# A hybrid decoder block on one core: attention's beginning in a written order, running sums as rows of the logits' product, and three smaller moves

## The chip, the cores and the metric

The kernel runs on one core of a Trainium2 chip. A core has a matrix engine (TensorE, PE in the profile, with its weight loads shown apart as PEld), a vector engine (DVE), an activation engine (ACT), a general engine (POOL), a queue engine that issues transfers (SP), and 16 DMA engines. Engines run their instructions in order and wait for each other by semaphores. The metric is the device time of one execution in microseconds; lower is better.

## The reference

One layer of a decoder block on 1024 tokens of width 1024, in float32. Cut to what matters here:

```python
def forgetting_attention(q, k, v, log_f):
    c = jnp.cumsum(log_f, axis=1)                       # running sum per head
    ...
    logits = jnp.einsum('bqhd,bkhd->bhqk', qi, k) * scale
    logits = logits + ci[..., None] - c_k
    logits = jnp.where(causal, logits, -jnp.inf)
    p = jax.nn.softmax(logits, axis=-1)
    return jnp.einsum('bhqk,bkhd->bqhd', p, v)

def chunked_spatial_gating(u, vg, v_gain, w_s, b_s):
    vg = rmsnorm(vg, v_gain.reshape(G, Dg))
    w = w_s * jnp.tril(jnp.ones((CHUNK, CHUNK)))
    mixed = jnp.einsum('gij,bnjgd->bnigd', w, vc) + b_s.T[None, None, :, :, None]
    return u * mixed

xn = rmsnorm(h, norm_mix_g);  proj = xn @ w_in          # q, k, v, u, gate, forget logits
att = forgetting_attention(q, k, v, log_sigmoid(forget + b_forget))
sg = chunked_spatial_gating(gelu(u), gelu(gate), ...)
h = h + concat([att, sg]) @ w_out
h = h + conv_ffn(rmsnorm(h), w_up, conv_w, conv_b, w_down)   # 1024 -> 2*2816 -> 1024
return rmsnorm(h, norm_final_g)
```

There are 8 attention heads of 64 and 8 gating groups of 64.

## The kernel before

**Numbers in two halves.** A float32 value is split into a rounded high part and the rest (`split_w`: ACT casts the high part, DVE or POOL subtracts). A product is then three products: high by high, high by low, low by high. Large products (512 columns a matmul) are in addition computed by Strassen-Winograd steps on halves (the names A11, S1 to S4, T1 to T4 and so on).

**Stages.** Gate and value projections come first, then queries and keys of head pairs (`qk_step`, four steps), the rest of the values (`tmul` and `tprod` into four accumulator banks `S`, lines 729 to 732), the spatial gate (`spatial`, line 679, called at 733), attention, the output product (`wmm`, line 1019), the up projection with convolution, the down projection, and the last norm (`finish`, line 1426).

**Order.** Python emits instructions in program order and a scheduler gives each engine its queue; it may let a ready instruction pass an earlier one that is not. Three devices restrict it. `Line` wraps ACT and DVE: while `on` is true every call is ordered behind the one before on that engine. `seq` chains TensorE's instructions in attention. `after` orders one instruction behind another.

**Spatial gate.** Eight groups, three matmuls each into one bank (lines 690 to 692); DVE adds the bias and multiplies by `u`, two instructions a group, one for each half of the tokens (sixteen of 128x256). `turn_sg(hf)` (line 699) then transposes a half of the result on TensorE into four banks (line 705), ACT casts the high part (707), DVE subtracts the low part (708). Those are the `G` tiles that the output product of the gate reads.

**Attention.** For head h and query tile j (128 queries against (j+1)x128 keys), `logits(h, j)` (line 776):
- POOL's `affine_select` (786) copies the running sums of the last 512 keys with the causal mask into the place of the result; for the other keys the sums are read from `cks`, a copy of the head's row on all 128 partitions.
- For each 512 keys two matmuls into one bank (793, 794): rows (q high, q low) by (k high, k low), and the same rows by (k low, k high). There are four such banks (tag "s").
- DVE adds the sums to the bank and takes the running minimum, one instruction for each 512 keys (796; the kernel keeps the logits negated, so the minimum is the softmax's maximum).
- ACT takes the exponential with the row sum (799).

`turn_p` transposes two key tiles of the result into a bank (812), ACT casts (813), DVE subtracts (814). `values` multiplies them with V (831) and adds the two halves (839, 840). `row_tail(h)` takes the reciprocal of the row sums on DVE (738), transposes it (739), copies it (740) and sends it through memory to be spread. `pair_half` multiplies a pair of heads with it on POOL (752 to 754) and splits the result for the output product.

A head is five steps of two transposed groups. In step s of head h the values of head h and the logits of head h+1 are computed (`NEXT`), and the transposes of the next step are emitted ahead. `FILLS` names the steps after which one **filler** is emitted: a token tile of the gate's part of the output product (`sg_out`, 12 matmuls, lines 873 to 875, sixteen in all), with its own load, addition (876) and store. Fillers use the four "b" banks, which the transposes and values use too. `head_loads(h)` issues a head's transfers two heads ahead; the output weights of attention are loaded and split on POOL by `wo_load` (898, 899) in head 7's program place, ordered behind selects and loads of head 6.

**Last norm.** `finish(tt, done)`: ACT takes the root of the mean square, DVE the reciprocal (1432), ACT scales one half of the row (1434), DVE the other half with the gain (1435), SP stores the tile (1437). It runs for tiles 4 to 7 after the last product.

Of the kernel before, what the change touches and what calls it, by code (L numbers as in the profile page):

```python
# [14 lines left out]
P = 128  # L15
# [5 lines left out]
FILLS = {(-1, j): 1 for j in (5, 3, 0)} | {(h, s): 1 for h in range(5) for s in ((0, 2, 4), (1, 3))[h % 2]}  # L21
# [44 lines left out]
def block_kernel(ctx: ExitStack, tc: tile.TileContext, xT, xtok, wuv, wv, wqk, wf, cpk, bfv,  # L66
# [76 lines left out]
    ncd = drm.tile([8, 1024], F32, name="ncd")  # L143
# [108 lines left out]
    def tmul(banks, w, n, k, first, apart=False):  # L252

        ops = [(m, c) for m in range(4) for c in range(3)]
        for m, c in sorted(ops, key=lambda o: (o[1] > 0, o)) if apart else ops:
            ms = slice(m * P, (m + 1) * P)
            xi, wi = ((0, 0), (0, 1), (1, 0))[c]
            pe.matmul(banks[m], xs(n, xi, k)[:, ms], w[:, wi, :], start=(first and k == 0 and c == 0),
                      stop=(k == 3 and c == 2), skip_group_check=True)
# [196 lines left out]
    def forget():  # L456
# [4 lines left out]
        bfb, z, e, rows = c[:, 136:144], c[:, 144:208], c[:, 208:272], c[0:64, 272:400]  # L461
        tri, ones, lh, ll = r[:, 0:P], r[:, P:2 * P], r[:, 256:320], r[:, 320:384]
# [7 lines left out]
        act.copy(ones, one128)  # L470
        dve.scalar_tensor_tensor(out=tri, in0=maskb, scalar=0.0, in1=ident, op0=ALU.is_gt, op1=ALU.add)
# [18 lines left out]
    def forget_sums(c, r, zr):  # L490
        sel, bfb, z, e, rows = c[0:64, 128:136], c[:, 136:144], c[:, 144:208], c[:, 208:272], c[0:64, 272:400]
# [25 lines left out]
        def turn():  # L517
            pe.transpose(ps[0:64, 192:320], z, ident)
            act.activation(rows, ps[0:64, 192:320], AF.Copy, scale=-1.0)
            sp.dma_start(out=ncd.rearrange("h (t p) -> (h t) p", p=P), in_=rows)  # L520
# [47 lines left out]
    def qk_step(i, qa, nxt):  # L568
# [22 lines left out]
        if i < 2:  # L591
            gate_part(0, 2 * i)
# [16 lines left out]
        emit(tq, qd, i, -0.125, (hi,))  # L609
        return qa  # L610
# [68 lines left out]
    def spatial():  # L679
# [5 lines left out]
        ws = [sb("wy", [P, 8, P], F32R) for _ in range(2)]  # L685
        split_w(wr, ws)
        for g in range(8):
# [5 lines left out]
            for hf in range(2):  # L693
                u3 = ut[hf][:, :, g * 64:(g + 1) * 64]
                dve.scalar_tensor_tensor(out=u3, in0=ps[:, hf * 256:(hf + 1) * 256].rearrange("p (t d) -> p t d", d=64),
                                         scalar=bs[:, g:g + 1], in1=u3, op0=ALU.add, op1=ALU.mult)

    def turn_sg(hf):

        for c in range(4):  # L700
            if hf == 0:
                sgT[c] = sb("G", [P, 2, 1024], F32R)
            ps = bank()
            for t in range(4):
                seq(pe.transpose(ps[:, t * P:(t + 1) * P], ut[hf][:, t, c * P:(c + 1) * P], ident))
            o = slice(hf * 512, hf * 512 + 512)
            act.copy(sgT[c][:, 0, o], ps)
            dve.tensor_tensor(out=sgT[c][:, 1, o], in0=ps, in1=f32(sgT[c][:, 0, o]), op=ALU.subtract)

    S = [sbank() for _ in range(4)]  # L710
    for k in range(4):
        tmul(S, w0[k], "T3", k, True)
        pool.tensor_tensor(out=wvr[k][:, 1, :], in0=wvr[k][:, 0, :], in1=wvr[k][:, 1, :], op=ALU.add)
    tprod(S, lambda k: wvr[k][:, 1, :], "B22", False)
    spatial()
    for m in range(4):
        evac_v(4 + m, S[m])

    act.activation(pad[:, 0:1], eps, AF.Exp)
    act.last = dve.last = None  # L720
# [7 lines left out]
    loads = [None] * 8  # L728
    exs = []
    rows = [None] * 8  # L730
    sels = [[] for _ in range(8)]

    def row_tail(h):
# [3 lines left out]
        rt = sb("t01", [8, P])  # L737
        dve.reciprocal(rs, rs)
# [6 lines left out]
    def pair_half(p, o):  # L745
# [4 lines left out]
        if p < 3:  # L750
            s = sels[2 * p + 3][o.start // 512 * 3:]
# [761 lines left out]
```

## Time and profile before

| what | value |
|---|---|
| time, median of 3 runs (range) | 1075.26 us (1074.52 to 1075.49) |
| the profiled execution's own time | 1075.26 us |
| its span, first to last instruction | 1073.5 us |
| granted TensorE clock, mean | 0.998 |
| ACT, POOL busy share | 53%, 23% |
| DMA moved | 160.80 MB, mean 150 GB/s |

A row of the timeline has the start, the length, the engine, the line, the operation, output from input with shapes, and in brackets the engine's idle time before it with what released it. Consecutive equal instructions are merged (x12). A row of the stretches has the length and then the busy time of PE, PEld, DVE, ACT and POOL (number of instructions), the granted clock, the DMA share and GB/s. Matmul ends are modelled, so a row can overlap its successor; the distance from start to start is the rate.

### The profile page before, as it was taken

The page shows a single profiled execution, that of the slowest core. Times are in us where ns is not written, and L with a number is a line of the kernel's source. Part 1 is how long each engine was busy: PE and PEld are TensorE (multiplying, and loading weights), DVE is VectorE, ACT ScalarE, POOL GpSimd, SP SyncE. Part 2 cuts the span into 40 slices and gives each one's busy share as a digit, 9 for nine tenths or more (in the row PEclk, how much of TensorE's full clock was granted, in tenths as well). Part 3 has the DMA queues.
Part 4 walks back from the last instruction along what each step waited for, and adds up shares of the span by engine and source line. Part 5 has one row for each costly group of instructions (what it writes and reads, how often), then busy time and mean ns, then how long its engine had stood idle before and what let it go on. Part 6 is the DMA issues. An engine that isn't in the chain of part 4 may idle for free.

```text
span 1073.5 us, 14486 instructions
## 1 busy us (share of the span) xinstructions
PE 1055.4 (98%) x5013; PEld 875.3 (82%) x5013; DVE 897.1 (84%) x1367; ACT 570.7 (53%) x985; POOL 245.6 (23%) x219
## 2 busy tenths in 40 slices
PE   9999999999999899999999999999999999999997
PEld 7888788778888788878888888888888888888886
DVE  5986798787877869999899988989988776898774
ACT  6666644466666755764444444444344444454653
POOL 0002134131316630054333333333322000000000
PEclk9999999999999999999999999999999999999999
DMA  9243267956547425132245413222331899433442
GB/s 339 96 137 100 69 159 213 266 189 204 179 167 235 130 89 197 68 117 91 101 135 170 164 69 128 99 99 98 107 118 48 289 323 323 123 94 97 143 123 96
DMA packets 66297, 160.80 MB, mean 150 GB/s; under 512 B 7976, under 2 KB 8240, under 8 KB 66224
## 3 DMA queue, kind: packets, MB, share of 16 engines
q1 hardware_dynamic: 65792, 159.32, 45.6%
q8 instruction: 39, 0.64, 0.2%
q10 hardware_dynamic: 432, 0.57, 0.1%
q14 instruction: 34, 0.28, 0.1%
HBM read 117.06 MB, written 42.80 MB: 149 GB/s over the span
## 4 chain that ended last, share of the span: by engine, by line
PE 74%; DVE 3%; DMA 2%; issue 1%; ACT 1%; POOL 0%; POOLq 0%; DVEq 0%; ACTq 0%; SPq 0%
PE k L1366 20%; PE qa L1114 11%; PE qc L1114 11%; PE qd L1114 11%; PE qb L1114 5%; PE pb L831 3%; PE pb L812 2%; PE pf L873 1%; PE ps L793 1%; PE pf L875 1%; PE ps L794 1%; PE pf L874 1%; PE pb L1023 1%; PE pb L1025 1%; PE pb L1024 1%
## 5 line engine op out<-in xcount | busy, mean ns | idle before, releaser
L1366 PE MATMUL k<-whb,wha 128*128 128x512 f32 x924 | 209.7, 389 | 0.0
L1366 PEld LDWEIGHTS k<-whb,wha 128*128 128x128 f32 x924 | 173.3, 188 | 36.2 <-DVE wha L160 0.2
L1114 PE MATMUL qc<-xT,whb 128*128 128x512 f32 x540 | 129.8, 389 | 0.0
L1114 PE MATMUL qa<-xB,wha 128*128 128x512 f32 x528 | 127.3, 390 | 0.0
L1114 PEld LDWEIGHTS qc<-xT,whb 128*128 128x128 f32 x540 | 101.3, 188 | 21.2 <-ACT whb L154 0.2
L1114 PEld LDWEIGHTS qa<-xB,wha 128*128 128x128 f32 x528 | 98.8, 188 | 20.8 <-DVE wha L160 0.4
L154 ACT CAST wha<-sg 128x512 fp32r<-128x512 f32 x77 | 47.8, 622 | 96.9 <-PE k L1366 86.4
L154 ACT CAST whb<-sg 128x512 fp32r<-128x512 f32 x82 | 50.6, 618 | 86.0 <-PE qc L1114 69.0
L160 DVE TENSOR_TENSOR wha<-sg,wha 128x512 fp32r<-128x512 f32 x77 | 52.8, 688 | 40.4 <-ACT wha L154 40.3
L1114 PE MATMUL qd<-xB,whb 128*128 128x512 f32 x264 | 63.9, 389 | 0.5 <-DVE h L1233 0.5
L1114 PE MATMUL qd<-xT,whb 128*128 128x512 f32 x264 | 63.6, 389 | 0.0
L1001 POOL TENSOR_TENSOR sg<-raw 128x512 f32<-128x512 f32 x20 | 31.2, 1562 | 136.5 <-DVE whb L160 75.7
L160 DVE TENSOR_TENSOR whb<-sg,whb 128x512 fp32r<-128x512 f32 x82 | 58.3, 711 | 4.4 <-ACT whb L154 4.3
L1114 PE MATMUL qb<-xT,whb 128*128 128x512 f32 x252 | 60.9, 389 | 0.0
L814 DVE TENSOR_TENSOR pt<-pb,pt 128x512 fp32r<-128x512 f32 (+1 forms) x80 | 49.9, 634 | 11.4 <-ACT pt L813 10.9
L1114 PEld LDWEIGHTS qd<-xB,whb 128*128 128x128 f32 x264 | 49.5, 188 | 11.2 <-issue 0.9
L1114 PEld LDWEIGHTS qd<-xT,whb 128*128 128x128 f32 x264 | 49.5, 188 | 10.3
L1114 PEld LDWEIGHTS qb<-xT,whb 128*128 128x128 f32 x252 | 47.3, 188 | 9.8
L813 ACT CAST pt<-pb 128x512 fp32r<-128x512 f32 (+1 forms) x80 | 42.4, 539 | 20.7 <-PE pb L812 13.5
L831 PE MATMUL pb<-pt,V 128*128 128x256 f32 x320 | 51.5, 285 | 0.9 <-DVE pt L814 0.8
L1004 POOL TENSOR_TENSOR sg<-sg,raw 128x512 f32<-128x512 f32 x20 | 33.4, 1670 | 64.3 <-DVE whb L160 64.3
L831 PEld LDWEIGHTS pb<-pt,V 128*128 128x128 f32 x320 | 44.1, 189 | 3.3 <-PE pb L812 1.1
(401 smaller groups left out, 2298.8 us busy)
## 6 DMA issues: line engine op xcount, KB each, us to landing
raw<-wup SPq DMA_DIRECT2D x44, 512.0 KB, 3.7
sg<-hx SPq DMA_DIRECT2D x77, 256.0 KB, 2.7
hx<-hs SPq DMA_DIRECT2D x44, 256.0 KB, 3.6
hx<-ca SPq DMA_DIRECT2D x35, 256.0 KB, 2.3
xT<-wdn SPq DMA_DIRECT2D x28, 256.0 KB, 4.0
raw<-wqk SPq DMA_DIRECT2D x8, 512.0 KB, 4.7
qd<-G SPq DMA_DIRECT2D x16, 256.0 KB, 3.2
kd<-G SPq DMA_DIRECT2D x16, 256.0 KB, 3.8
```

The lines of the kernel that those rows point to most:

```text
L154: act.copy(h, src)
L160: return eng.tensor_tensor(out=l, in0=src, in1=f32(h), op=ALU.subtract)
L793: seq(pe.matmul(ps[:, 0:e - c], A[:, qs], B[:, c:e], start=True, stop=False))
L794: seq(pe.matmul(ps[:, 0:e - c], A[:, qs], B2[:, c:e], start=False, stop=True))
L812: seq(pe.transpose(ptr[:, c:c + P], tj[jj][:, k * P:(k + 1) * P], ident))
L813: act.copy(pt[:, 0, 0:w], ptr[:, 0:w])
L814: dve.tensor_tensor(out=pt[:, 1, 0:w], in0=ptr[:, 0:w], in1=f32(pt[:, 0, 0:w]), op=ALU.subtract)
L831: seq(pe.matmul(po[0][:, oo:oo + n], lhs, pt[:, s, o:o + n], start=(k == 0 and s == 0), stop=(s == 1 and half)))
L1001: pool.tensor_tensor(out=s[0], in0=a21, in1=a22, op=ALU.add)
L1004: pool.tensor_tensor(out=s[3], in0=s[1], in1=a12, op=ALU.add)
L1114: pe.matmul(ps, w[:, wi, ks], xb[:, xi, k, :], start=(first and n == 0), stop=(n == 11), skip_group_check=True)
L1366: pe.matmul(banks[bk + m], xh[:, xi, ms], wh[:, wi, :], start=(first and p_ == 0 and n == 0), stop=(p_ == NP - 1 and n == 2), skip_group_c ...
```

## The change

**Values' bank order.** The first eight blocks of the values' product no longer go bank by bank for each k: banks 0 to 2 take k = 0 and 1 first, then bank 3.

**Gate's norm.** `gate_part(0, 2)` (a square on ACT, a reduction and two 1024-wide products on DVE) moves from the middle of `qk_step(1)` to its end.

**Running sums as rows.** The negated sums are stored as high and low rows, and a row pair of ones beside them. A logit's two matmuls become (q high, q low) by (k high, k high), and (q high, 1, 1) by (k low, sums high, sums low), 66 rows deep. The product of the low parts of q and k is left out. `cks`, its broadcast load and POOL's selects go. A constant mask (bfloat16: zeros, and at its end the triangle of large numbers) is added instead. The bank pool is laid out anew for attention: four "b" banks and two places "L" of two banks each; a tile's logits, whatever their width, take one place, and one DVE instruction reads them.

**The beginning.** Loads of head 0 are issued ahead of the values' last product. From `spatial` to the first logits the order of ACT and DVE is written out. The V parts are taken from the banks ahead of the gate; DVE multiplies the first half of the tokens, ACT adds the bias to the second half and POOL multiplies it; the splits of the filler's weights stand between the groups, on ACT and POOL.

**Heads.** Fillers stand after steps 0, 2, 4 of head 0 and 1, 4 of heads 1 to 5. The reciprocal of `row_tail` is taken ahead of the second minimum of the next head, its transposes after the step's first values. POOL's work on pairs and output weights is ordered behind no select any more. After attention the bank pool is laid out a third time, and the first products of the output go half by half.

**Last root.** For tile 6, `finish` scales its half on POOL instead of ACT.

```diff
-FILLS = {(-1, j): 1 for j in (5, 3, 0)} | {(h, s): 1 for h in range(5) for s in ((0, 2, 4), (1, 3))[h % 2]}
+FILLS = {(-1, j): 1 for j in (5, 3, 0)} | {(h, s): 1 for h in range(6) for s in ((0, 2, 4) if h == 0 else (1, 4))}
...
+        sp.dma_start(out=oned.rearrange("s (t p) -> (s t) p", p=P), in_=f32(ones[0:16, :]))
...
+            rh, rl = r[0:64, 0:P], r[0:64, P:2 * P]
+            act.activation(rh, ps[0:64, 192:320], AF.Copy, scale=-1.0)
+            dve.scalar_tensor_tensor(out=rl, in0=ps[0:64, 192:320], scalar=-1.0, in1=f32(rh),
+                                     op0=ALU.mult, op1=ALU.subtract)
+            for s, t in enumerate((rh, rl)):
+                sp.dma_start(out=ncd[s].rearrange("h (t p) -> (h t) p", p=P), in_=f32(t))
...
-        if i < 2:
-            gate_part(0, 2 * i)
+        if i == 0:
+            gate_part(0, 0)
...
+        if i == 1:
+            gate_part(0, 2)
...
+        act.on = dve.on = True
         split_w(wr, ws)
+        act.activation(pad[:, 0:1], eps, AF.Exp)
+        for m in range(4):
+            evac_v(4 + m, S[m])
+        tmp = [sb("pt", [P, 4, 256]) for _ in range(2)]
         for g in range(8):
...
+            dve.scalar_tensor_tensor(out=u[0], in0=v3(ps[:, 0:256]), scalar=bs[:, g:g + 1], in1=u[0],
+                                     op0=ALU.add, op1=ALU.mult)
+            t = tmp[g // 4][:, g % 4, :]
+            act.activation(t, ps[:, 256:512], AF.Identity, bias=bs[:, g:g + 1])
+            pool.tensor_tensor(out=u[1], in0=v3(t), in1=u[1], op=ALU.mult)
+            if g in parts:
+                parts[g]()
...
+    for k, ms_ in ((0, range(3)), (1, range(3)), (0, (3,)), (1, (3,)), (2, range(4)), (3, range(4))):
+        tmul(S, w0[k], "T3", k, True, ms_=ms_)
...
+        sp.dma_start(out=f32(ab[:, 0, :]), in_=qd[h].rearrange("s d t -> (s d) t"))
+        for s in range(2):
+            sp.dma_start(out=f32(ab[s * 64:s * 64 + 64, 1, :]), in_=kd[h, 0])
+        sp.dma_start(out=f32(a2s[0:64, hh, :]), in_=qd[h, 0])
+        if h < 2:
+            sp.dma_start(out=f32(a2s[64:66, hh, :]), in_=oned)
+        sp.dma_start(out=f32(b2s[64:66, hh, :]), in_=ncd[:, h, :])
+        loads[h] = sp.dma_start(out=f32(b2s[0:64, hh, :]), in_=kd[h, 1])
...
+    head_loads(0)
     tprod(S, lambda k: wvr[k][:, 1, :], "B22", False)
...
+    spatial({3: early_split, 5: early_split})
...
+    psa.release()
+    psa = tc.alloc_tile_pool(name="psb", bufs=4, space=bass.MemoryType.PSUM, reuse_waits="tile")
+    def place():
+        return psa.tile([P, 1024], F32, tag="L", bufs=2, name=nm("pl"))
...
+            seq(pe.matmul(ps[:, c:e], A[:, qs], B[:, c:e], start=True, stop=False))
+            seq(pe.matmul(ps[:, c:e], A2[:, qs], B2[:, c:e], start=False, stop=True))
...
+        m = dve.tensor_tensor_reduce(out=places[h, i][jj], in0=ps[:, 0:n], in1=msk[:, 1024 - n:1024], scale=1.0,
+                                     scalar=lim[:, 0:1], op0=ALU.add, op1=ALU.min, accum_out=mn)
+        if h and j == 6:
+            after(tc, m, recips[h - 1])
...
-    turn_sg(0)
-    for j in range(7, -1, -1):
+    for c in range(4):
+        ps = turn_sg(0, c)
+        sg_hi(0, c, ps)
+        sg_lo(0, c, ps)
+        if c % 2:
+            early_split()
+    for j in (7, 6):
+        logits_mm(0, j, firsts[j])
+    pts = [turn_sg(1, c) for c in range(4)]
+    for c in range(4):
+        sg_hi(1, c, pts[c])
+    m7 = logits_min(0, 7, firsts[7])
+    sg_lo(1, 0, pts[0])
+    sg_lo(1, 1, pts[1])
+    m6 = logits_min(0, 6, firsts[6])
+    sg_lo(1, 2, pts[2])
+    logits_exp(0, 7, m7)
+    logits_exp(0, 6, m6)
+    logits(0, 5)
+    sg_lo(1, 3, pts[3])
+    act.on = dve.on = False
...
+            if s == 1 and c == (h == 7):
+                row_tail(h)
...
+    psa.release()
+    psa = tc.alloc_tile_pool(name="psc", bufs=4, space=bass.MemoryType.PSUM, reuse_waits="tile")
...
-    for tt in first:
-        for hf in range(2):
+    for hf in range(2):
+        for tt in first:
             wmm(tt, hf, banks8[tt, hf], (0, 1, 2))
...
+        if tt == 6:
+            pool.tensor_tensor(out=y[tt][:, done], in0=y[tt][:, done], in1=r.to_broadcast((P, 512)), op=ALU.mult)
+        else:
+            act.activation(y[tt][:, done], y[tt][:, done], AF.Copy, scale=r)
```

180 lines of the change are left out of this document (82 added, 98 removed).

## The prediction

> **What bounds the kernel now.** I read the page's first block, the busy time by stretch, then the timelines of each engine around the stretches where TensorE is not full.
>
> ```profile
> span 1073.5 us, 14486 instructions
> PE 1055.4 (98%) x5013; PEld 875.3 (82%) x5013; DVE 897.1 (84%) x1367; ACT 570.7 (53%) x985; POOL 245.6 (23%) x219
> ...
> 500.00:520.00 20.00, 20.00 (x90) 16.42 (x89) 16.41 (x18) 9.11 (x14) 6.79 (x5) 1.00 0.23 79
> ```
>
> TensorE sets the end: 18.1 us of idle in the whole span. In a full stretch 90 matmuls of 512 columns take 20 us, 0.222 us each, so one filler (12 of them) is worth 2.67 us. From about 400 us to the last matmul PE is full, so what is won before 400 us moves the end by as much. Almost all idle lies in two places, the beginning of attention and the heads. The beginning on PE, and what ACT, DVE and POOL do beside it (start, us, engine, line, idle before):
>
> ```profile
> 194.07 3.69 PE L258 MATMUL ps<-wy,x 128*128 128x512 f32 x15 [0.83 <-DVE G L44]
> ...
> 203.04 5.63 PE L258 MATMUL ps<-wy,t 128*128 128x512 f32 x24
> ...
> 219.39 1.81 PE L705 MATMUL pb<-ident,A 128*128 128x128 f32 x12
> 221.36 0.63 PE L705 MATMUL pb<-ident,A 128*128 128x128 f32 x4 [0.15 <-DVE A L44]
> ...
> 223.56 1.91 PE L705 MATMUL pb<-ident,A 128*128 128x128 f32 x16
> 225.25 0.50 PE L793 MATMUL ps<-x 128*128 128x512 f32 x1
> ...
> 227.74 0.50 PE L873 MATMUL pf<-whl,G 128*128 128x512 f32 x1 [1.31 <-DVE G L708]
> ...
> 238.01 1.80 PE L812 MATMUL pb<-ident,t 128*128 128x128 f32 x15
> ```
> ```profile
> 212.11 2.73 ACT L44 ACTIVATE V<-ps,rstd 128x512 fp32r<-128x512 f32 x4 [4.45 <-PE ps L258]
> 220.03 0.59 ACT L707 CAST G<-pb 128x512 fp32r<-128x512 f32 x1 [5.19 <-PE pb L705]
> ...
> 236.52 0.49 ACT L799 ACTIVATE gg<-gg,mn 128x256 f32<-128x256 f32 x1
> ```
> ```profile
> 202.34 1.28 DVE L44 TENSOR_TENSOR wy<-raw,wy 128x512 fp32r<-128x512 f32 x2
> ...
> 214.86 6.35 DVE L44 SCALAR_TENSOR_TENSOR A<-pb,cp,A 128x256 f32<-128x256 f32 x16
> ...
> 225.79 0.74 DVE L796 CUSTOM_DVE_ANT_0 t<-ps,t,mn 128x512 f32<-128x512 f32 x1
> ...
> 226.46 0.61 DVE L796 CUSTOM_DVE_ANT_0 t<-ps,t,mn 128x384 f32<-128x384 f32 x1
> ...
> 227.00 2.48 DVE L708 TENSOR_TENSOR G<-pb,G 128x512 fp32r<-128x512 f32 x4
> ```
>
> The gate's 16 products (6.35 us) run on DVE alone while ACT idles 5.19 us. All later DVE work is pushed back: the second set of low parts (L708) starts only at 227.00, behind the minima. The first filler needs one of the four banks that those transposes hold, and starts 1.31 us late, when the first L708 is done.
>
> The heads: one row from each row-sum transpose (L739) to the next (length; PE, PEld, DVE, ACT, POOL busy).
>
> ```profile
> 244.76:263.88 19.12, 18.97 (x126) 16.90 (x125) 15.02 (x38) 12.23 (x27) 3.41 (x8) 1.00 0.64 208
> 263.88:286.91 23.03, 22.31 (x139) 19.08 (x137) 19.29 (x48) 15.62 (x34) 6.30 (x11) 1.00 0.54 173
> 286.91:306.34 19.43, 19.03 (x126) 16.90 (x125) 15.01 (x38) 12.77 (x29) 6.71 (x12) 1.00 0.65 208
> 306.34:348.08 41.74, 41.01 (x264) 35.98 (x262) 32.07 (x82) 26.54 (x58) 17.36 (x28) 1.00 0.60 193
> 348.08:364.40 16.32, 13.97 (x104) 12.39 (x102) 14.95 (x41) 12.77 (x29) 7.03 (x10) 1.00 0.50 148
> 364.40:380.89 16.49, 14.33 (x103) 12.68 (x104) 13.13 (x35) 13.53 (x30) 11.77 (x14) 1.00 0.26 81
> ```
>
> The rows hold 2, 3, 2, 5 (two heads), 0 and 0 fillers; the last has six matmuls of the output product instead. Less 2.67 us a filler and 0.222 us a matmul, a head takes 13.78, 15.02, 14.09, 14.20 twice, 16.32 and 15.16 us. Against the best, 13.78, the rows lose 0, 1.24, 0.31, 0.84, 2.54 and 1.38: **6.3 us**. Heads without fillers lose most: DVE is 92% busy there and PE waits for it.
>
> **Part 1, the beginning: minus 1.9 us.** The values' bank order takes up the 0.83 us wait, for only the fourth bank was late. But what is late next is the split of the following product, done on DVE at 202.34 plus half of 1.28, just when PE arrives at 203.04 now: I credit 0.2 (bounds 0 and 0.83). The gate's second half moves to ACT and POOL. ACT's 256-column pass is not in the trace; between half of a 0.59 cast and the 0.49 exponential it is about 0.4, eight are 3.2 us beside 5.4 us of products (24 by 0.222), and two early splits (1.2) fit too. POOL's product is priced by these rows:
>
> ```profile
> L1002 POOL TENSOR_TENSOR sg<-sg,raw 128x512 f32<-128x512 f32 x20 | 34.6, 1728 | 47.8 <-issue 45.2 <-DVE whb L160 1.8 <-POOL sg L1001 0.7
> ...
> L160 POOL TENSOR_TENSOR whl<-raw,whl 128x512 fp32r<-128x512 f32 x4 | 5.0, 1298 | 0.0
> ```
>
> Half of 1.30 or of 1.73 for 256 columns: 0.65 to 0.86. I take 0.65, since the 1.30 row is of this place. From 215.3 (ACT's last V copy ends at 214.84, plus one pass) eight products and two splits end at 215.3 + 5.2 + 2.6 = 223.1, two more splits at 225.7. PE: gate transposes from 219.39 (1.7), the first two logits (1.7), so 222.8; the second transposes end at about 223.6, one wait for POOL in them. DVE after its eight gate products (220.1): four low parts behind ACT's casts to 223.7, minimum of tile 7 to 225.0, first low part of the second set 225.6, which frees the filler's bank. So the first filler starts near 225.7 instead of 227.74: 2.0 us. With 0.86 and 1.73 the last split ends at 229.1; its weights are needed 2.0 us into the filler, so it starts at 227.1: 0.6 us. Behind it, tile 5's place waits for tile 7's minimum and the last three logits alternate over two places: I take off 0.3. Sum 0.2 + 2.0 - 0.3 = 1.9 (0.3 to 2.8). The forced order queues ACT's exponentials behind the last casts; only the transposes at 238.01 wait for them, some 10 us on.
>
> **Part 2, logits and fills: minus 3.6 us.** The product count stays; rows 66 deep instead of 128 are priced at 0. POOL's 64 selects go, off the path. The minimum reads PSUM 1024 wide in one instruction: from start to start the 512 row takes 0.67 us and the 384 row 0.54, so 128 columns cost 0.13 and an instruction as such 0.15; a head saves four of these, 0.6 us of DVE; bound 0 if two banks in one instruction cost what two do. Loads for a head fall from 2.0 to 1.5 MB but go from five to six transfers, on an SP queue that the fillers' loads share; the DMA share is 0.5 to 0.65, I price them at 0. Fillers now stand in heads 0 to 5, two in each row above, but with two unfilled steps in a row. Heads 1 to 5 lost 4.9 us together; at 0.35 each, as heads 2 to 4 lose, it is 1.75: gain 3.2. Head 6 stays unfilled; the reciprocal is placed before the second minimum, which removes this wait but leaves the later one:
>
> ```profile
> 364.40 0.27 PE L739 MATMUL pb<-ident,rs 128*8 128x128 f32 x1 [0.98 <-DVE rs L738]
> ...
> 375.20 0.63 PE L812 MATMUL pb<-ident,H 128*128 128x128 f32 x4 [1.40 <-DVE pt L814]
> ```
>
> I take 0.4. Output weights can now be split only after the last filler, one head later:
>
> ```profile
> 343.60 0.61 POOL L898 CAST whl<-raw 128x512 fp32r<-128x512 f32 x1 [2.30 <-PE pf L875]
> 344.30 1.29 POOL L899 TENSOR_TENSOR whl<-raw,whl 128x512 fp32r<-128x512 f32 x1
> ```
>
> Eight pairs of these are 15.2 us, and the last pair of heads adds 6 operations of 0.6 to 1.3, 6.4 us: from about 356 to 378, before the output product at about 382. Hidden with some 4 us to spare; the outer loop over halves asks for the second halves later still. Bounds of this part: +1.5 (below) to -6.3.
>
> **Part 3, the gate's norm: 0.** It leaves DVE around 144 for a place one step later:
>
> ```profile
> 144.24 3.95 DVE L44 TENSOR_TENSOR G<-G,gms 128x1024 f32<-128x1024 f32 x2
> ...
> 160.00:180.00 20.00, 19.95 (x89) 16.20 (x88) 17.53 (x24) 7.71 (x14) 9.94 (x6) 1.00 0.71 195
> ```
>
> PE does not wait there now, so nothing is won; the 2.47 us that DVE idles at 160 to 180 covers it, else up to 1 us.
>
> **Part 4, the last root: plus 0.5 us.**
>
> ```profile
> 1067.45 0.75 DVE L1435 SCALAR_TENSOR_TENSOR y<-y,ssf,gfb 128x512 f32<-128x512 f32 x1
> ...
> 1068.01 0.70 ACT L1434 ACTIVATE y<-y,ssf 128x512 f32<-128x512 f32 x1
> 1068.62 0.28 ACT L1431 ACTIVATE ssf<-ssf 128x1 f32<-128x1 f32 x1
> ```
> ```profile
> 1069.50:1070.00 0.50, 0.00 (x0) 0.00 (x0) 0.38 (x1) 0.35 (x1) 0.00 (x0) 0.90 0.92 377
> ...
> 1072.00:1072.50 0.50, 0.00 (x0) 0.00 (x0) 0.00 (x0) 0.00 (x0) 0.00 (x0) 0.50 0.24 90
> ```
>
> The last tile's root waits on ACT for the scaling of tile 6; without it the root starts 0.52 us earlier, at 1068.10. But the stores of both tiles (0.5 MB each, some 400 GB/s) run without a break from about 1069.5 to 1072.1: the end follows tile 6, whose data start 0.8 us after its scaling ends at 1068.71. On POOL that scaling starts at 1067.5 and takes 1.30 to 1.73 us: end 1068.8 to 1069.2, so 0.1 to 0.5 later. DVE scales the tile's other half (L1435) from SBUF at that moment, as in the 1.73 row, so I take 0.5 (bounds 0 and 0.8, the latter if POOL first waits for L1435 to end at 1068.2). [...]
>
> **The sum.** -1.9 - 3.6 + 0 + 0.5 = -5.0 us on the profiled span of 1073.5, so 1068.5. That execution took 1075.26 us in all, the median of the three runs shown, with 1.76 us around the span: **1070.3 us**.
>
> **Rivals.**
> (a) *The fills, stretched thin, let DVE set the heads, and two wide places tie PE to it.* Now four single banks let the narrow logits run ahead; afterwards each takes one of two places, so PE waits for the minimum two tiles back. Heads 5 and 6 lost 3.9 us in ten unfilled steps in a row, 0.39 a step. After the change 15 unfilled steps in heads 1 to 5 stand in pairs and 5 in head 6: at 0.6 a step (half as much again, for the places) 12 us against 6.3 now, +5.7; with the beginning and the tail +4.3: 1079.6 us, slower. It decides once DVE is over some 2.2 us behind PE, the time from one logit to the next but one (two transposes, two value groups). For it: DVE is 92% busy in the unfilled head. Against: DVE has 0.6 us less a head, and in filled heads it is 79% busy (15.02 of 19.12).
> (b) *Gains cancel.* POOL is late at the beginning (0.86 and 1.73: gain 0.6, less 0.3), the 20 unfilled steps lose 0.39 each (7.8, so +1.5) and the tail costs 0.8: +2.0, so 1077.3 us, just inside no change. For it: the contended POOL row. Against: the 1.30 row is of the same place.
> (c) *All waits go.* Beginning 2.8, heads 6.3, tail 0: -9.1, so 1066.2 us. For it: everything asked of POOL has time to spare once the selects are gone. Against: ACT carries 13.5 us of a head of 13.8, so unfilled head 6 can't run clean.
> (d) *The change doesn't do what it says:* the order of engines left free around the forced stretch (the norm, the splits of the values' product) comes out later and eats the beginning; -3.6 + 0.5 + 1 = -2.1, so 1073.2 us.
>
> **Chances.** Mine 0.60, (a) 0.14, (b) 0.10, (c) 0.10, (d) 0.06. About 0.2% (2.15 us: below 1073.1, above 1077.4) can be told from no change. Mine and its spread (1067.5 to 1073.5) is faster with 0.56 and same with 0.04; (c) is faster with 0.10; (d) splits 0.03 faster, 0.03 same; (b) splits 0.06 same and 0.04 slower; (a) is slower with 0.14. Together faster 0.69, same 0.13, slower 0.18. The range goes from rival (c) to the end of rival (b), 1066.5 to 1077.0, and leaves out (a) and a little on both ends.
>
> **What would show it.** Right: the first filler at 225 to 227 us, its wait gone or under 0.5; DVE's gate products at half of 6.35 us; 64 minima instead of 96 pieces; the row-sum transposes of heads 0 to 6 some 18.7 to 19.5 us apart; no 0.98 us wait at the reciprocal; output weights split before the output product, with PE full from there. Tail: last scaling on POOL over 1.3 us, tile 6's store later than now. Wrong: waits of the logits' products on the minima (rival a), the second gate transposes waiting for POOL beyond 225 us (b), a wait on an output weight's split, or heads at over 20 us.

## The result and the profile after

| | before | after |
|---|---|---|
| time, median of 5 runs each (range) | 1075.26 us (1074.52 to 1075.49) | 1085.35 us (1085.05 to 1085.47) |
| ratio, 95% interval | | 1.0087 (1.0075 to 1.010) |
| span of the profiled execution | 1073.5 us | 1083.5 us |
| granted TensorE clock, mean | 0.998 | 0.995 |

Predicted were 1070.3 us, in a range of 1066.5 to 1077.0: the change is slower by 10.1 us, 8 us beyond the end of the range. First, from the page of the kernel after, the span and the busy time of the engines; then TensorE's waits in the order of their sums (us in total, number of waits, longest).

```profile
span 1083.5 us, 14308 instructions
PE 1057.9 (98%) x5013; PEld 876.5 (81%) x5013; DVE 887.5 (82%) x1292; ACT 572.9 (53%) x992; POOL 229.2 (21%) x170
```
```profile
PE pb L878 <- DVE pt L880: 6.2, 7, 1.0
PE pb L719 <- ACT wy L51: 3.0, 1, 3.0
PE ps L259 <- DVE wy L44: 1.7, 1, 1.7
...
PE pb L738 <- ACT pt L51: 1.1, 1, 1.1
PE pl L841 <- DVE mn L854: 0.9, 2, 0.7
```

DVE is 10 us less busy and TensorE's count of matmuls is the same; the time went into waits and into slow matmuls. Where, is seen in TensorE's timeline around the rows that the prediction shows of before:

```profile
192.92 5.62 PE L259 MATMUL ps<-wy,x 128*128 128x512 f32 x24
...
205.89 5.51 PE L259 MATMUL ps<-wy,t 128*128 128x512 f32 x23 [1.69 <-DVE wy L44]
...
219.87 0.80 PE L719 MATMUL pb<-H,wy 128*128 128x512 f32 x1 [3.03 <-ACT wy L51]
221.72 0.63 PE L719 MATMUL pb<-H,wy 128*128 128x512 f32 x1
...
226.74 0.39 PE L719 MATMUL pb<-H,wy 128*128 128x512 f32 x1
227.42 0.39 PE L719 MATMUL pb<-H,wy 128*128 128x512 f32 x1
...
230.03 1.96 PE L738 MATMUL pb<-ident,A 128*128 128x128 f32 x16 [1.09 <-ACT pt L51]
...
236.19 0.39 PE L922 MATMUL pf<-whl,G 128*128 128x512 f32 x1
...
244.35 0.33 PE L841 MATMUL pl<-x 128*128 128x128 f32 x1 [0.73 <-DVE mn L854]
...
247.42 1.80 PE L878 MATMUL pb<-ident,t 128*128 128x128 f32 x15
```

The first head transposes start at 247.42 instead of 238.01, so 9.4 of the 10.0 us of span are lost ahead of the heads. Two things are new there.

**The spatial gate starts 3.03 us late and then runs slowly.** The order of the weights' way is SP (load), POOL (select), ACT (cast), TensorE:

```profile
206.14 3.33 SPq L693 DMA_DIRECT2D raw<-wos  x2
210.02 0.33 SPq L705 DMA_DIRECT2D pt<-wsp  x1
```
```profile
217.65 1.09 POOL L706 TENSOR_SCALAR_AFFINE_SELECT pt<-pt 128x1024 f32<-128x1024 f32 x1 [17.83 <-DMA pt<-wsp]
```
```profile
218.77 1.04 ACT L51 CAST wy<-pt 128x1024 fp32r<-128x1024 f32 x1 [8.37 <-POOL pt L706]
219.83 1.28 ACT L51 ACT_TABLE_LOAD   x1
...
221.24 2.40 ACT L51 ACTIVATE V<-ps,rstd 128x512 fp32r<-128x512 f32 x4
225.10 1.70 ACT L51 ACTIVATE pt<-pb,cp 128x256 f32<-128x256 f32 x4 [1.46 <-DVE A L51]
```

SP issues the load at 210.02; before, it issued it at 175.79:

```profile
175.79 0.67 SPq L682 DMA_DIRECT2D pt<-wsp  x1
```

Counted in the two traces, it was the 78th transfer that SP issued and is now the 105th, behind the whole of head 0's loads and the fillers' weights. After the 3.03 us of idle the granted clock is at 0.50. Stretches of 1 or 2 us of the kernel after (length; PE, PEld, DVE, ACT, POOL busy; clock; DMA share; GB/s):

```profile
220.00:222.00 2.00, 1.96 (x4) 1.15 (x5) 1.13 (x2) 1.99 (x4) 0.00 (x0) 0.50 1.02 225
...
226.00:227.00 1.00, 1.00 (x5) 0.79 (x5) 0.35 (x2) 1.00 (x3) 1.00 (x2) 0.83 0.00 0
```

A group of three spatial products takes 0.68 us at the full clock (226.74 to 227.42). The first five groups take 6.87 us (219.87 to 226.74) instead of 3.4, so 3.5 us go to the clock.

**DVE is late from 160 us on.** The gate's norm (square on ACT; reduction, reciprocal and two products on DVE) ran from 135 to 148 us before; now, on ACT and then on DVE:

```profile
155.38 1.06 ACT L44 ACTIVATE pt<-G 128x1024 f32<-128x1024 f32 x1
```
```profile
156.48 1.22 DVE L44 TENSOR_REDUCE gms<-pt 128x16 f32<-128x1024 f32 x1 [0.75 <-ACT pt L44]
...
160.82 4.54 DVE L44 TENSOR_TENSOR G<-G,gms 128x1024 f32<-128x1024 f32 x2
```
```profile
160.00:180.00 20.00, 19.42 (x87) 15.78 (x85) 20.00 (x23) 7.35 (x14) 11.38 (x6) 1.00 0.36 109
```

DVE has no idle time left in that stretch, and TensorE waits for its splits (0.58 us at 168.35, 1.69 at 205.89). The two products take 4.54 us here, beside sums on POOL that take up to 2.27 us each; where POOL is idle beside them, two such products take 2.36 (b_gate below, at 161.70) and 2.35 (the norm's first part in this kernel, at 122.49). The later wait isn't the norm's alone: DVE idles 1.83 us at 193.38, between the two, and in the runs below that start from this kernel and have the norm at its former place, that wait is still 0.63 to 1.64 us.

The table splits the span of each kernel at three points of TensorE: the start of the values' product, the start of the first head transposes, and the end of the last matmul (in the kernel after 1069.83 + 6.05). "Beginning" and "heads and rest" are the distances between them, "tail" is the rest of the span. The names are those of the experiments below. (In the kernel before, the values' last product and the call of `spatial` stand on lines 711 to 715.) The first product of the queries and keys, which lies ahead of all the places edited, starts between 103.62 and 104.77 us in these traces; so less than about 1 us in the start of the values' product is not by itself an effect of an edit.

| kernel | time (us) | values' product starts | beginning | heads and rest | tail | span |
|---|---|---|---|---|---|---|
| before | 1075.26 | 191.04 | 46.97 | 828.60 | 6.89 | 1073.5 |
| after | 1085.35 | 192.92 | 54.50 | 828.46 | 7.62 | 1083.5 |
| a_wsp | 1080.00 | 193.25 | 48.73 | 828.08 | 7.64 | 1077.7 |
| a_rows | 1084.03 | 192.84 | 54.73 | 827.90 | 7.63 | 1083.1 |
| a_gate | 1075.32 | 192.06 | 46.46 | 827.83 | 7.55 | 1073.9 |
| a_wrg | 1074.91 | 190.79 | 46.81 | 827.86 | 7.54 | 1073.0 |
| a_t01 | 1075.85 | 192.40 | 46.17 | 827.96 | 7.57 | 1074.1 |
| b_gate | 1078.91 | 194.97 | 46.74 | 828.49 | 6.90 | 1077.1 |
| g_tail | 1074.66 | 190.51 | 46.86 | 827.89 | 7.14 | 1072.4 |
| g_f24 | 1071.59 | 190.50 | 47.46 | 824.78 | 7.16 | 1069.9 |
| b_tail | 1075.74 | 191.12 | 46.84 | 828.51 | 7.33 | 1073.8 |
| g_fills | 1074.49 | 191.10 | 47.90 | 827.61 | 7.19 | 1073.8 |
| h_best | 1070.80 | 191.52 | 46.24 | 824.97 | 7.17 | 1069.9 |

### The profile page after: what moved, and what is told of

Its sections match the earlier page's. It is cut to its first block, busy times and chain, and to the rows that moved or that the text cites. A ratio compares the mean times of both kernels' runs of the same rounds, so it can differ in the third digit from the quotient of the medians.

```text
span 1083.5 us, 14308 instructions
## 1 busy us (share of the span) xinstructions
PE 1057.9 (98%) x5013; PEld 876.5 (81%) x5013; DVE 887.5 (82%) x1292; ACT 572.9 (53%) x992; POOL 229.2 (21%) x170
## 4 chain that ended last, share of the span: by engine, by line
PE 73%; DVE 3%; ACT 3%; DMA 1%; issue 1%; POOL 0%; SPq 0%; ACTq 0%; DVEq 0%; POOLq 0%
PE k L1437 19%; PE qa L1185 11%; PE qc L1185 11%; PE qd L1185 11%; PE qb L1185 5%; PE pb L897 2%; PE pb L878 2%; PE pf L922 1%; PE pf L924 1%; PE pf L923 1%; PE pb L1094 1%; PE pb L1096 1%; PE pb L1095 1%; PE pl L841 1%; PE pl L842 1%
```

## The experiments

Names with a_, g_ and h_ start from the kernel after, those with b_ from the kernel before. Runs of the kernel before on the same chip gave 1075.44 us beside the first four, 1075.41 beside the next four, 1075.98 beside the last three.

### a_wsp: the spatial weights' load issued early

The added lines stand ahead of the values' product; the same lines are taken out of `spatial`.

```diff
+    wr = sb("pt", [P, 8, P])
+    sp.dma_start(out=wr, in_=wsp)
+    pool.affine_select(out=wr, in_=wr, pattern=[[0, 8], [1, P]], ...)
     S = [sbank() for _ in range(4)]
```

> The changed kernel, with the load of the spatial weights (and POOL's select on it) issued ahead of the values' product, so ahead of head 0's loads on SP's queue, as it stood before the change. Theory A (the late load is the largest loss): in the changed kernel the first spatial matmul waits 3.03 us for the weights' cast, and the granted clock that then falls to 0.50 stretches the following 24 products and the transposes from 5.4 to 10.2 us. With the load early the wait goes, the clock stays at 1.00, the first spatial matmul stands near 216.8 us instead of 219.87, the first filler near 228.5 instead of 236.2; the time falls by 6 to 8 us to about 1078.3. Rival: another wait takes the place of this one, since ACT's order is forced (table load 1.28 us, four V copies 2.40 us ahead of the bias passes): the matmuls start early but the banks of the gate come free no sooner, the gain is under 2.5 us, about 1083.5. Second rival: the clock falls anyway, through the idle that is left; gain 3 us, about 1082.

Measured 1080.0 us: 5.35 us won of the 7 expected. The wait at the first spatial product (now at 217.84) is gone, and the clock stays at 1.00, as the stretch of the first fence shows; DVE's lateness stays (second fence, TensorE):

```profile
215.00:220.00 5.00, 5.00 (x24) 4.14 (x23) 3.28 (x6) 2.79 (x5) 0.00 (x0) 1.00 1.03 293
```
```profile
207.05 5.51 PE L259 MATMUL ps<-wy,t 128*128 128x512 f32 x23 [1.76 <-DVE wy L44]
224.55 1.97 PE L734 MATMUL pb<-ident,A 128*128 128x128 f32 x16 [1.08 <-ACT pt L51]
```

So the late load is the largest single loss, about half of the whole.

### a_rows: the running sums' rows back in c

```diff
-            rh, rl = r[0:64, 0:P], r[0:64, P:2 * P]
+            rh, rl = c[0:64, 272:400].bitcast(F32R), c[0:64, 0:P].bitcast(F32R)
```

> The changed kernel, with the two 64x128 rows of the running sums written into free columns of the tile c, as before the change, instead of the tile r. Theory A: of the two buffers named gg the one of r then comes free when r's last transpose is done, so POOL's sum S2 of the queries' and keys' product starts near 130 us instead of 136.23, and the two waits of the L403 matmuls at 138.2 to 139.8 us (0.74 and 0.34) go: 1.1 us less, about 1084.3. Rival: the sum is late for another reason (POOL's own order, the transfer of the rows): the waits stay, no change, 1085.3.

Measured 1084.03 us, the number that I expected, but by the ratios to before (1.0077, 1.0062 to 1.0092, against 1.0087, 1.0075 to 1.010) it isn't told apart from the kernel after, and the spans differ by only 0.4 us. First POOL's sum, then TensorE:

```profile
130.01 1.63 POOL L426 TENSOR_TENSOR gg<-raw,raw 128x512 f32<-128x512 f32 x1
```
```profile
168.26 2.99 PE L403 MATMUL qc<-V,whl 128*128 128x512 f32 x12 [1.84 <-DVE G L44]
```

The sum starts at 130.01 instead of 136.23, the two waits near 139 us are gone: the buffer's part is right. But the next wait grows from 0.58 to 1.84 us, and the values' product starts at 192.84 against 192.92. What is gained on TensorE is given back to DVE, which sets the pace at 168 us in this kernel. What is won after that (the wait at 205 us is 1.21 instead of 1.69) is lost to the late spatial weights: the first spatial product waits 4.00 us instead of 3.03.

### a_gate: the norm's second part at its former place

```diff
-        if i == 0:
-            gate_part(0, 0)
+        if i < 2:
+            gate_part(0, 2 * i)
...
-        if i == 1:
-            gate_part(0, 2)
```

> The changed kernel, with the second part of the gate's norm at its former place, one step earlier. Theory A: the moved norm fills DVE in 160 to 180 us (20.00 of 20 us busy, 17.53 before the change), and the split of the matrix G comes 0.58 us late for the L403 matmul at 168.35; at the former place DVE has its slack back, the wait falls to 0.05, and the time by 0.5 us, about 1084.8. Rival: the norm makes DVE as late in the step before it (a wait near 150 us takes its place), no change or up to 1 us slower: 1085.3 to 1086.3.

Measured 1075.32 us: 10.0 us won instead of 0.5. Theory and rival were both far off. This one edit takes the whole loss away: ratio to before 0.9997 (0.9988 to 1.0007). The load of the spatial weights is now the 80th transfer of SP's queue (105th in the kernel after), and SP's timeline shows when it was issued:

```profile
176.65 0.67 SPq L703 DMA_DIRECT2D pt<-wsp  x1
```

No line of the load itself was touched. So the norm's place and the load's place on SP hang together; a_t01 below asks how.

### a_wrg: all three

> The changed kernel with all three: spatial weights loaded early, rows of the running sums in c, second part of the norm at its former place. Theory A: the three losses stand one behind the other on TensorE, so the gains add: 7.0 + 1.1 + 0.5 = 8.6 us, about 1076.8, which is still over the kernel before by the tail's 0.7 and the split of B22's factor 1.7. Rival: what is won ahead of the heads is lost in them, since head 1's loads or DVE are late next: under 4 us in all, 1081 or more.

Measured 1074.91 us: better than expected, because the gain of a_gate was underrated; the gains don't add (10.0 + 5.4 + 1.3), since a_gate has the early load already. The times don't tell it apart from a_gate (1075.32). In the traces the values' product starts 1.27 us earlier (190.79 against 192.06); 0.36 of that was there at 104 us already, so the rows in c are worth some 0.9 us, which is also the difference of the spans. They show here, since DVE no longer holds TensorE at 168 us.

### a_t01: the norm stays moved, its square lies elsewhere

```diff
-        sq = sb("pt", [P, 2, 512])
+        sq = sb("t01" if (hf, t) == (0, 2) else "pt", [P, 2, 512])
```

> The changed kernel with the second part of the norm left where the change put it, but its square (128x1024) in the buffer named t01 instead of one of the three named pt. Theory B: three buffers pt are shared by the halves of the queries' and keys' product, the norm's squares and the spatial weights; the moved square holds one of them at the moment when the planner would place the weights' load, so it comes 72nd on SP's queue instead of 56th, behind head 0's loads and the filler's weights. With the square elsewhere the load is 56th again, issued near 177 us: the 3.03 us wait at the first spatial matmul and the clock of 0.50 behind it go, as when the load was moved by hand (1080.0 us); DVE's backlog from the moved norm stays. About 1080, 1079 to 1081.5. Rival: the norm's time on DVE is all that matters, the load is late only because of it: no gain, 1084.5 or more. Second rival: the buffer is the whole loss of the norm's move: 1075.5, as with the norm at its former place.

Measured 1075.85 us: the second rival, not my theory. The load is the 80th transfer again, as in a_gate (the 72nd and 56th of my expectation are not the traces' count). The square now runs at 196.57 on ACT, later than ever, and TensorE waits for nothing there:

```profile
175.61 0.68 SPq L705 DMA_DIRECT2D pt<-wsp  x1
```
```profile
196.57 1.06 ACT L44 ACTIVATE t<-G 128x1024 f32<-128x1024 f32 x1 [0.98 <-DVE G L44]
```

With nothing changed but the square's buffer, the norm leaves the stretch 155 to 165 us, DVE has its slack back (18.23 of 20 us busy in 160 to 180), and the weights' load is early: that the square's place in the three buffers pt ties the two together is shown. The other traces agree. Where the moved square takes a buffer pt, the load is issued at 185.28 us (b_gate below), at 186.93 (a_wsp, moved by hand) and at about 210 (after, a_rows); where the norm is at its former place or its square lies elsewhere, at 174.7 to 176.7. (By which rule the planner, the scheduler that orders the queues, chooses the places was not followed up.) This run undoes both effects at once; a_wsp parts them by difference only: 5.35 us come with the load, and some 4.2 (1080.0 to 1075.85; 3.6 by the spans) with what is left of the norm's place. Of that, 2.8 us are three waits of a_wsp for DVE that a_t01 doesn't have (0.56 at 168.67, 0.46 at 197.95, 1.76 at 207.05); that the norm's time on DVE causes all three is not shown.

### b_gate: the norm's move alone, in the kernel before

```diff
-        if i < 2:
-            gate_part(0, 2 * i)
+        if i == 0:
+            gate_part(0, 0)
...
         emit(tq, qd, i, -0.125, (hi,))
+        if i == 1:
+            gate_part(0, 2)
```

> The kernel before, with one part of the change alone: the second part of the gate's norm moved one step later. Head loads do not stand ahead of the spatial weights there, so their load stays early. Theory B: what remains of the norm's move is the backlog on DVE (20.00 of 20 us busy in 160 to 180 us in the changed kernel), which in the changed kernel with the early load still costs 4.7 us against the norm at its former place (1080.0 against 1075.3); the values' splits come late here too: 2 to 5 us slower, 1077.5 to 1080.5. Rival (the prediction's own step): the 2.47 us that DVE idles at 160 to 180 us covers it: no change, 1075.4, at most 1 us.

Measured 1078.91 us, ratio 1.0029 (1.0017 to 1.0041): the step that I priced at nothing costs 3.5 us by itself, as much as theory B had it, but in one piece and not by theory B's mechanism. TensorE, and stretches around it:

```profile
169.34 2.88 PE L402 MATMUL qa<-V,whl 128*128 128x512 f32 x12
174.28 4.52 PE L402 MATMUL qd<-t,whl 128*128 128x512 f32 x12 [2.06 <-DVE G L44]
178.64 2.89 PE L402 MATMUL qb<-H,wy 128*128 128x512 f32 x12
```
```profile
172.00:174.00 2.00, 0.22 (x1) 0.00 (x0) 2.00 (x3) 0.00 (x0) 0.38 (x1) 1.00 0.00 0
174.00:175.00 1.00, 0.72 (x2) 0.65 (x3) 1.00 (x3) 0.00 (x0) 0.12 (x1) 0.58 0.22 49
...
176.00:178.00 2.00, 2.00 (x7) 1.54 (x7) 1.98 (x3) 0.85 (x2) 0.48 (x1) 0.60 0.47 146
```

A wait of 2.06 us for DVE, and then the clock near half (0.58, 0.50 and 0.60 in the stretches from 174 to 178): the row of 12 matmuls takes 4.52 us instead of 2.88. 2.06 + 1.64 = 3.7, about the 3.9 us by which the values' product starts later than before (194.97 against 191.04; 0.4 of it was there at 104 us already). But DVE isn't full here: it is busy for 17.69 of 20 us in 160 to 180, nearly as before (17.53). It idles itself, for ACT's cast of a sum of weights that POOL has finished late. ACT and DVE in this run, then ACT in the kernel before:

```profile
169.46 0.62 ACT L44 CAST wy<-gg 128x512 fp32r<-128x512 f32 x1 [4.78 <-POOL gg L425]
```
```profile
170.12 1.12 DVE L44 TENSOR_TENSOR wy<-gg,wy 128x512 fp32r<-128x512 f32 x1 [1.83 <-ACT wy L44]
```
```profile
165.17 0.62 ACT L44 CAST wy<-gg 128x512 fp32r<-128x512 f32 x1 [1.71 <-POOL gg L425]
```

On POOL's queue a sum for the values' product (L715) now stands ahead of the two sums that this cast needs, and it starts only at 164.13, when the norm's second product ends on DVE (161.70 + 2.36); before, the two sums came first, at 161.76 and 163.52. So by this trace the move costs time here through a sum that comes late on POOL, and not by filling DVE. The load of the spatial weights comes later here too (185.28 instead of 175.79), but early enough: the spatial products don't wait.

### g_tail: in addition, the last root's scaling on ACT

```diff
-        if tt == 6:
-            pool.tensor_tensor(out=y[tt][:, done], in0=y[tt][:, done], in1=r.to_broadcast((P, 512)), op=ALU.mult)
-        else:
-            act.activation(y[tt][:, done], y[tt][:, done], AF.Copy, scale=r)
+        act.activation(y[tt][:, done], y[tt][:, done], AF.Copy, scale=r)
```

> The changed kernel with the three repairs (spatial weights early, rows of the sums in c, norm at its former place: 1074.91 us) and in addition tile 6's last scaling on ACT as before the change. Theory: POOL's scaling took 1.55 us and stretched the DVE instruction beside it to 0.99 us, and from the last matmul to the end of the span it is 7.6 us instead of 6.87; undone, 0.7 us less: about 1074.2. Rival: the end is set by the stores of tiles 6 and 7 in either case, no change, 1074.9.

Measured 1074.66 us against 1074.91 for a_wrg; the times don't tell them apart (their ranges overlap). The tail in the trace does: 7.14 us against 7.54.

### b_tail: POOL's scaling alone, in the kernel before

The edit of g_tail the other way round, put into the kernel before.

> The kernel before, with one part of the change alone: tile 6's last scaling on POOL. Theory: POOL's scaling beside DVE's of the other half takes some 1.5 us and ends later than ACT's 0.70 us; tile 6's store and with it the end come 0.4 to 0.8 us later; from the last matmul to the end of the span 7.3 to 7.6 us instead of 6.87, the time 1075.9 to 1076.2. Rival: the order of the stores changes with it and the loss is nil: 6.9 us, 1075.4. The reading is the distance in the profile; the time itself is hardly told apart.

Measured 1075.74 us, ratio 0.9999 (0.999 to 1.0008), not told apart; the tail is 7.33 us against 6.89. Part 4 costs 0.4 us in the traces, in both directions of the test.

### g_f24: fillers after steps 2 and 4

```diff
-... (0, 2, 4) if h == 0 else (1, 4) ...
+... (0, 2, 4) if h == 0 else (2, 4) ...
```

> As g_tail, with the two fillers of heads 1 to 5 after steps 2 and 4 instead of 1 and 4. Theory: in every head TensorE loses 0.99 us at the first transposes of step 4, emitted with step 3: their bank waits for DVE's low part, which waits for ACT's cast behind two exponentials; it is the second of two unfilled steps with two minima each. A filler between them covers the wait: up to 5 x 0.99, about 1070 (1069 to 1072). Rival: the wait goes to the new unfilled pair (steps 0 and 1, the widest minima and exponentials, 1.28 and 1.15 us): 1074 or slower.

Measured 1071.59 us, ratio 0.9965 (0.9952 to 0.9977): 3.1 us won over g_tail. First the kernel after at the place of the wait (DVE, ACT and TensorE in order of time), then two rows of heads of after and two of g_f24, from one row-sum transpose to the next:

```profile
282.36 0.94 ACT L862 ACTIVATE t<-t,mn 128x768 f32<-128x768 f32 x1 [1.69 <-DVE mn L854]
...
283.30 0.81 ACT L862 ACTIVATE t<-t,mn 128x640 f32<-128x640 f32 x1
...
284.11 0.83 ACT L879 CAST pt<-pb 128x384 fp32r<-128x384 f32 x2
...
284.60 1.02 DVE L880 TENSOR_TENSOR pt<-pb,pt 128x384 fp32r<-128x384 f32 x2 [0.32 <-ACT pt L879]
...
285.30 1.09 PE L878 MATMUL pb<-ident,t 128*128 128x128 f32 x8 [0.99 <-DVE pt L880]
```
```profile
334.95:354.81 19.86, 18.87 (x126) 16.83 (x125) 15.09 (x31) 12.81 (x30) 0.00 (x0) 1.00 0.54 157
...
374.68:389.19 14.51, 12.97 (x99) 11.48 (x97) 11.23 (x26) 12.49 (x31) 12.78 (x15) 1.00 0.53 174
```
```profile
265.88:284.99 19.11, 18.96 (x126) 16.89 (x125) 14.64 (x31) 14.39 (x34) 8.58 (x8) 1.00 0.51 149
284.99:304.85 19.86, 19.10 (x126) 16.90 (x125) 15.24 (x32) 13.70 (x30) 2.62 (x3) 1.00 0.61 179
```

In the kernel after the casts of step 2 stand behind two exponentials on ACT; the low part follows, and TensorE's next transposes wait 0.99 us for the bank, in each of the five heads with fillers after steps 1 and 4. With a filler in between, four of the five rows fall from 19.87 to 19.1 us. One (284.99) stays at 19.86; it holds a wait of 0.62 us for ACT's copy of the row sums, and why only this one does stays open. The new unfilled pair costs nothing, against the rival.

### g_fills: the fillers at their places of before

```diff
-... {(h, s): 1 for h in range(6) for s in ((0, 2, 4) if h == 0 else (1, 4))}
+... {(h, s): 1 for h in range(5) for s in ((0, 2, 4), (1, 3))[h % 2]}
```

> As g_tail (1074.66 us), with the fillers of the heads where they stand before the change: after steps 0, 2, 4 of even heads and 1, 3 of odd ones, heads 0 to 4, none in heads 5 and 6. It tells the new logits from the new places of the fillers. Theory (the logits' change does gain, the new places of the fillers give it back): each of the rows with fillers 1 and 4 holds one wait of 0.99 us, while the unfilled head 6 takes 14.24 us of TensorE's time, 0.3 less than a filled one net of its fillers (14.53); with no two unfilled steps between fillers the rows of heads 1 to 4 lose at most 0.4 each and heads 5 and 6 take 14.3 each: about 1072 (1071 to 1073). Rival: the logits' change gains nothing, heads 5 and 6 take 16 and 15 us as before the change: 1075 or more.

Measured 1074.49 us: above my theory's 1071 to 1073 and just under the rival's 1075, so neither came as stated. Heads 5 and 6, unfilled, take 14.75 and 14.51 us in the trace instead of 16.32 and 15.16 (0.4 us of the last is only where the row ends, see part 2 below): the new logits do help there, against the rival. Rows with three fillers take 23.25 and 22.83, with a wait of 1.00 us for a bank at a filler, and the beginning is 1.0 us longer than in g_tail, the B22 block (the second half of the values' product, from 203.82 on in the kernel after) waiting 1.64 us: the planner again made another order there. The heads and the rest are 0.3 us shorter than in g_tail, so neither set of places is better; (2, 4) is better than both.

### h_best: what the runs point to

The edits of a_rows, a_t01, g_tail and g_f24 together, on the kernel after.

> Meant to beat both kernels: the changed kernel with the rows of the sums in c, the moved norm's square in the buffer t01 (its place and the load of the spatial weights as in the change), tile 6's last scaling on ACT, fillers after steps 2 and 4 of heads 1 to 5. g_f24 with the norm moved back took 1071.59 us, with waits of 1.25 us at the B22 block; with the square in t01 there was no wait at that block (a_t01). Theory: 0.5 to 1.2 us less, about 1070.7. Rival: the norm, which then runs near 196 us, and the selects' places meet again: 1071.6 or more.

Measured 1070.8 us, ratio to before 0.9952 (0.994 to 0.9965): faster than both kernels, by 5 us than before and by 14.5 than after. It isn't told apart from g_f24 (both spans are 1069.9).

## Why the prediction was wrong, step by step

**Part 3, the gate's norm, "0 ... else up to 1 us": this step failed, and it is two thirds of the error**, 10.0 of 15.05 us; without it the time (1075.32, a_gate) lies inside the range. I wrote that "the 2.47 us that DVE idles at 160 to 180 covers it". The norm's DVE work was in the row that I quoted: 3.95 us for the products alone, and the reduction of 1.2 us beside it. 5 us don't go into 2.47, and in the kernel after DVE is busy for the whole stretch. I also took TensorE's lack of a wait for cover, without asking what stands behind the norm on DVE: the splits that TensorE needs next. And I followed the step's instructions, but not its buffer: the square takes one of the three buffers pt, and the load of the spatial weights needs one. Measured: 10.0 us in the changed kernel (a_gate), 3.5 in the kernel before (b_gate), some 0.5 with the square in another buffer (a_t01 against a_gate). Of the 10.0, 5.35 came with the load issued early. How the rest divides between DVE's time and the order of the other queues stays open: in b_gate it was a late sum on POOL.

**Part 1, the beginning, minus 1.9.** The 0.83 us wait for the fourth bank is gone, and the filler's wait of 1.31 is gone, as predicted: from the gate transposes to the first filler it is 6.16 us (230.03 to 236.19) instead of 8.35, 2.2 us less against my 2.0. The prices behind it held (POOL's product of 256 columns 0.71 us against 0.65, ACT's pass 0.43 against 0.4). What I sized wrong stands around it. The split that I named as late next costs 0 (a_t01) to 1.76 us (a_wsp), by the order on DVE. The gate transposes themselves, which I let start as before, wait 1.09 us for a bank that ACT's bias pass holds; and the two places cost 0.73 us, where I took off 0.3. With the norm out of the way the beginning is 0.5 (a_gate) to 0.8 us (a_t01) shorter, not 1.9. Transfers I looked at only as bytes and number ("I price them at 0"), and only for the heads; that the load of the spatial weights moved back by 34 us (175.79 to 210.02) was a matter of its place on SP's queue, which no term of the sum held.

**The buffer of the running sums** was not in my sum at all. It costs some 0.9 us at the start of the values' product (a_gate against a_wrg), hidden in the kernel after by DVE and the late load.

**Part 2, logits and fills, minus 3.6: it came to minus 0.1.** At "0.35 each" I assumed that a row loses by the number of unfilled steps. It loses by which step: rows with fillers after 1 and 4 take 19.87 us, 14.53 net of two fillers, 0.75 over the best. So heads 1 to 5 lose 3.75 us where I had 1.75. With fillers after 2 and 4 four of them take 13.76 net, and the heads and the rest are 3.8 us shorter than before (g_f24): that my 3.6 comes near it is luck, for I had it for other places. Unfilled head 6 took 14.24 (a_gate) to 14.51 us. That looks less than the 14.8 that I implied, but its row covers less work: the row-sum transposes now stand behind the first values and logits of their step (2.18 us of matmuls in the kernel before), in head 7 behind both values (1.77 us). With that 0.4 it is 14.65 to 14.9, as I had it. The reciprocal's wait is gone, but right behind the last head's row sums, at 390.35, there is a new one of 0.89 us for ACT's copy of them, in a_gate and g_f24 as well.

**Part 4, the last root, plus 0.5.** Right: 0.4 by both tests (the tail of the kernel after is 0.7 longer, but some 0.3 of that stays with the scaling on ACT, g_tail). After, on POOL and DVE:

```profile
1076.81 1.55 POOL L1507 TENSOR_TENSOR y<-y,ssf 128x512 f32<-128x512 f32 x1 [248.45 <-DVE ssf L1503]
```
```profile
1076.72 0.75 DVE L1510 SCALAR_TENSOR_TENSOR y<-y,ssf,gfb 128x512 f32<-128x512 f32 x1
...
1077.92 0.99 DVE L1510 SCALAR_TENSOR_TENSOR y<-y,ssf,gfb 128x512 f32<-128x512 f32 x1
```

The bound of 0.8, by which POOL first waits for DVE's L1435 to end (L1510 here), was not reached: by the trace DVE's instruction on the same tile ran from 1076.72 to 1077.47, and POOL's started beside it at 1076.81. POOL's ran until 1078.36, and DVE's from 1077.92 took 0.99 us instead of 0.75: 0.24 us longer, where waiting for POOL's end would have made it 0.44 longer (the times of POOL's instructions are rough).

**The rivals.** (d) named the right kind, an order of free engines that comes out later, and even the norm, but at 1 us and 6 in 100. (a) had the side right and the mechanism wrong: in the heads only one wait for a minimum is left, 0.21 us in head 6; the waits are for the banks of the transposes, and the heads didn't get longer. (b)'s late POOL didn't come: the second gate transposes don't wait.

## What to carry to other kernels

A moved step moves its buffer as well: list for each buffer name who takes the next buffer in turn, above all a load that is issued long ahead. Sum the moved instructions against the idle time of the new place, and ask what is queued behind them. Where a planner orders the queues, compare the places of the transfers, and of the sums on the other engines, before pricing "the same work" at nothing. And a filler is worth what the wait at its step is, so its place counts more than the number.

## What was not expected of the hardware

The granted clock fell to 0.50 after idle times of 2.06 us (b_gate), 3.03 us (after) and 4.00 us (a_rows, first spatial product), and by the shares of the stretches it stayed there for 3.4, 6.8 and 3.4 us; after 1.76 us (a_wsp) and 1.84 us (a_rows, at 168 us) it stayed at 1.00. So a wait of 2.06 us cost 3.7 us, and the wait of 3.03 about 6.5 (with the 3.5 of the five slow groups). In these three traces the slow stretch doesn't grow with the idle time: after the 4.00 us two products still ran at full clock (1.00 in 220 to 221 us, then 0.58 in 221 to 222) before it fell, and the 24 spatial products lost only some 1.8 us to the clock (8.61 us from first to last, less 5.44 for the products at full clock and 1.40 for two waits among them).
